# Adaptive max pooling on one core: which of 128 runs each partition loads, and how far apart the runs lie

## The chip, the cores and the metric

The kernel runs on one core of a Trainium2 chip. The metric is the device time of one execution in microseconds (us); the kernel before has a median of 334.78 us over 3 runs (334.77 to 335.02). One execution was also taken by the hardware profiler, and all views quoted here are of that one. Engines appear there as DVE (VectorE, which does the maxima), SPq and ACTq (the queues of SyncE and ScalarE, which here only start transfers) and POOL (GpSimd, which does nothing here beyond four constants). DMA stands for the core's 16 DMA engines. A load brings data from HBM (DRAM) into SBUF, a store takes results back. A KB in the profile's list of transfers is 1024 bytes, an MB in its totals is a million.

## The reference

```python
# x: (32, 256, 4096) float32, output_size = 256
for i in range(output_size):
    start = int(i * length / output_size)
    end = int((i + 1) * length / output_size)
    result[:, :, i] = np.max(x[:, :, start:end], axis=-1)
```

4096 / 256 = 16, so each output is the maximum of 16 neighbouring floats. Input and output are both contiguous, so the whole task is this: 32 * 256 * 256 = 2,097,152 windows of 64 B lie one after the other in DRAM, and the output is one float for each, in the same order. 134.2 MB are read and 8.4 MB written.

## The kernel before, in words

Each of the 128 partitions pools 2,097,152 / 128 = 16,384 windows. They are taken in two groups. Group A gives each partition 128 + 8 * 1024 + 1020 = 9340 windows, group B the other 7044. Within a group the windows are cut into 128 runs of equal length, one run per partition. In the kernel before, `group` (L66 to L73) gives partition p run p: its pattern `(p n) w -> p (n w)` makes run p begin p pitches behind the group's start, where the pitch is the length of a run, 9340 * 64 B = 597,760 B = 2335 blocks of 256 B in group A and 7044 * 64 B = 1761 such blocks in group B.

A run is loaded in pieces ("chunks"), the same piece of all 128 runs in one transfer, so that a chunk of 1024 windows is 128 rows of 64 KiB, one row for each partition. Group A is loaded from its end towards its beginning: a chunk of 128 windows first (`FIRST`, the load of L87), then eight of 1024 and one of 1020 (`CHUNK - LESS`; the loads of L96). Group B follows with six chunks of 1024 and a last one, `last`, which has 900 windows. The last chunk's length follows from `LESS`, since the two groups together must cover 16,384 windows.

The chunks go into `ring`, an SBUF buffer that holds two of them plus two gaps of 152 windows. Loads take the two halves in turn. A chunk is pooled by two instructions of `pooled` (L53 to L60, the instruction itself is on L56), one on 872 windows and one on 152; the order of the two and the gap let the next load of the same half start when the first of them is done. The maxima go into `kept`, another SBUF buffer, which holds all results but those of the last chunk; those are written into a part of `ring` (`last_kept`).

All loads are started by SP, in program order, each when the half that it fills is free. Behind the loads SP starts two stores (L117): the first with all of group A, 9340 floats per partition, the second with the first 6144 floats per partition of group B. The results of the last chunk, 900 floats per partition, are stored from the ScalarE queue (L114) when the last maximum is there. No engine's order is left to a planner here: every queue runs its instructions in the order in which the program writes them, and only semaphores make it wait.

The buffers of one transfer are given as two patterns, one for DRAM and one for SBUF. In the kernel before both count 128 rows in their outermost dimension.

## Time and profile before

| what | value |
|---|---|
| median of 3 runs | 334.78 us |
| span of the profiled execution | 333.1 us |
| DVE busy | 276.5 us, 83% of the span |
| DMA packets and bytes | 2880 packets, 142.61 MB |
| mean rate over the span | 428 GB/s |
| queue started by SP: share of 16 engines' span | 98.8% |
| queue started by ScalarE: share of 16 engines' span | 0.3% |
| mean time of a pooling instruction on 872 windows | 14.686 us |
| the same on 152 windows | 2.676 us |
| the same on the last chunk's 900 windows | 15.143 us |

The median is 1.7 us above the span of the profiled execution, since the span counts only from the first to the last instruction. The page gives each engine's busy time, a row of digits with the busy tenths in 40 equal slices of the span, the DMA queues with their share of the time of all 16 engines, the chain of work that ended last, the costliest groups of instructions with the idle time in front of them, and the transfers by the line that starts them, with the time from the start of the issuing instruction to the landing of the last byte. In that last list a transfer that stands in a queue behind others has that wait in its time.

### The profile page before, as it was taken

To read this page: it belongs to the slowest core of one execution; us is meant where nothing else is said; L and a number is where in the kernel's file an instruction comes from. 1 tells how busy PE (TensorE), PEld (TensorE's weight loads), DVE (VectorE), ACT (ScalarE), POOL (GpSimd) and SP (SyncE) were. 2 spreads that over 40 slices of the span, in tenths; PEclk is the share of its full clock that TensorE was granted. 3 is DMA by queue.
4 is the path that set the end of the run, shared out by engine and by line. 5 is a ranking of instruction groups with operands and counts; after the bars stand their busy time and mean duration, and the time that the engine had idled before them with its cause. 6 is when DMAs were issued, how large, how long until landed. Compare 5 with 4: busy or idle time off the path is not lost.

```text
span 333.1 us, 113 instructions
## 1 busy us (share of the span) xinstructions
DVE 276.5 (83%) x32; POOL 0.2 (0%) x4
## 2 busy tenths in 40 slices
DVE  2009979797997979799797979979797998979993
POOL 0000000000000000000000000000000000000000
DMA  9898989899898989899898989899898989899997
GB/s 378 378 504 378 504 378 504 378 449 433 378 504 378 504 378 504 378 441 441 384 494 377 504 378 504 378 456 425 386 496 378 504 378 504 378 458 443 393 395 330
DMA packets 2880, 142.61 MB, mean 428 GB/s; under 512 B 320, under 2 KB 320, under 8 KB 448
## 3 DMA queue, kind: packets, MB, share of 16 engines
q1 hardware_dynamic: 2736, 142.15, 98.8%
q10 hardware_dynamic: 144, 0.46, 0.3%
HBM read 134.22 MB, written 8.39 MB: 428 GB/s over the span
## 4 chain that ended last, share of the span: by engine, by line
DMA 57%; DVE 36%; DVEq 5%; issue 0%; SPq 0%
DMA ring<-in_x_dram 57%; DVE kept L56 36%; DVEq L148 5%; SPq L87 0%
## 5 line engine op out<-in xcount | busy, mean ns | idle before, releaser
L56 DVE TENSOR_REDUCE kept<-ring 128x152 f32<-128x2432 f32 (+3 forms) x31 | 261.4, 8473 | 51.5 <-DMA ring<-in_x_dram 51.5
L56 DVE TENSOR_REDUCE ring<-ring 128x900 f32<-128x14400 f32 x1 | 15.1, 15143 | 0.0
L134 POOL MEMSET const-bfloat16-1.0<- 128x1 bf16 x1 | 0.1, 103 | 0.0
L134 POOL MEMSET const-uint8-127<- 128x1 uint8 x1 | 0.1, 102 | 0.0
L134 POOL MEMSET const-float32-0.0<- 128x1 f32 x1 | 0.1, 100 | 0.2 <-issue 0.2
L134 POOL MEMSET const-float32-1.0<- 128x1 f32 x1 | 0.1, 99 | 0.0
## 6 DMA issues: line engine op xcount, KB each, us to landing
ring<-in_x_dram SPq DMA_DIRECT2D x1, 8160.0 KB, 23.9
ring<-in_x_dram SPq DMA_DIRECT2D x1, 7200.0 KB, 21.7
out_dram<-kept SPq DMA_DIRECT2D x1, 4670.0 KB, 32.4
out_dram<-kept SPq DMA_DIRECT2D x1, 3072.0 KB, 18.2
ring<-in_x_dram SPq DMA_DIRECT2D x1, 1024.0 KB, 4.7
out_dram<-ring ACTq DMA_DIRECT2D x1, 450.0 KB, 4.2
ring<-in_x_dram SPq DMA_DIRECT2D x14, 24.0
```

The costliest lines, as they stand in the source:

```text
L56: nc.vector.reduce_max(out=dst, in_=ring[:, at * W : (at + n) * W].rearrange("p (n w) -> p n w", w=W), axis=mybir.AxisListType.X,)
L134: nc = _bacc.Bacc("TRN2", target_bir_lowering=False, num_devices=1)
L148: with _tile.TileContext(nc) as tc:
```

## The change

Three things change together. `LESS` becomes 32: group A's last chunk has 992 windows in place of 1020, and the last chunk of group B has 928 in place of 900. With that a run of group A has 9312 windows, a pitch of 2328 blocks of 256 B in place of 2335, and a run of group B has 7072, a pitch of 1768 blocks in place of 1761. And `group` cuts the 128 runs into 8 sets of 16: its pattern is now `(j i n) w -> i j (n w)` with i counting 16 and j counting 8. The tile's side of each transfer still counts 128 partitions in order, so that partition 8 i + j takes run 16 j + i. Partitions 0 to 7 take runs 0, 16, 32 and so on up to 112, partition 8 takes run 1. Loads and stores both use it, so each result goes back to where its window was. `by_run` returns what it is given.

In the instructions the DRAM side of a load was 128 rows by 16384 floats; now it is 16 by 8 rows by 16384 floats, while the SBUF side is 128 by 1 by 16384. The number, order and waits of the instructions on each engine stay as they were.

```diff
-    LESS = 4
+    LESS = 32
+    RUNS = 16
...
+    def by_run(tile_rows):
+
+        return tile_rows
...
-            xw[span].rearrange("(p n) w -> p (n w)", p=P),
-            ow[span].rearrange("(p n) -> p n", p=P),
+            xw[span].rearrange("(j i n) w -> i j (n w)", i=RUNS, n=n),
+            ow[span].rearrange("(j i n) -> i j n", i=RUNS, n=n),
...
-            xn = xg[:, a * W : (a + n) * W]
+            xn = xg[:, :, a * W : (a + n) * W]
...
-                    out=ring[:, CHUNK * W : (CHUNK + n) * W], in_=xn
+                    out=by_run(ring[:, CHUNK * W : (CHUNK + n) * W]), in_=xn
...
-                nc.sync.dma_start(out=ring[:, at * W : (at + n) * W], in_=xn)
+                nc.sync.dma_start(
+                    out=by_run(ring[:, at * W : (at + n) * W]), in_=xn
+                )
...
-        stores.append((og[:, 0:full], kept[:, base : base + full]))
+        stores.append((og[:, :, 0:full], by_run(kept[:, base : base + full])))
...
-    nc.scalar.dma_start(out=og[:, full : full + last], in_=last_kept)
+    nc.scalar.dma_start(out=og[:, :, full : full + last], in_=by_run(last_kept))
```

## The prediction

> **What bounds the kernel now.** I read the page's busy tenths and queues first, to see whether an engine or the transfers fill the span.

> ```profile
> DVE  2009979797997979799797979979797998979993
> DMA  9898989899898989899898989899898989899997
> DMA packets 2880, 142.61 MB, mean 428 GB/s; under 512 B 320, under 2 KB 320, under 8 KB 448
> q1 hardware_dynamic: 2736, 142.15, 98.8%
> q10 hardware_dynamic: 144, 0.46, 0.3%
> ```

> The 16 DMA engines have something to move for 98.8 + 0.3 = 99.1% of the span; DVE has holes. The packets tell how a transfer is cut: the ScalarE queue carried one store, of 128 rows, in 144 packets, so 128 rows and 16 more, one for each engine. An engine thus has 8 rows of every transfer. Next, the table by stretches, cut where DVE's work on a chunk begins:

> ```profile
> core 0: us, DVE busy (x) POOL busy (x), PEclk, DMA share, GB/s
> 24.78:295.62 270.84, 241.84 (x28) 0.00 (x0) 1.00 1.00 433
> 312.82:327.99 15.17, 15.14 (x2) 0.00 (x0) 1.00 1.00 431
> 327.99:333.10 5.11, 0.00 (x0) 0.00 (x0) 1.00 0.59 244
> ```

> For 14 chunks on end the DMA share is 1.00 at 433 GB/s, and while only stores move (from 312.82) 1.00 at 431. So each engine moves 433 / 16 = 27.1 GB/s, into SBUF and out of it alike. Last, the waits, the timeline and the landings:

> ```profile
> DVE kept L56 <- DMA ring<-in_x_dram: 51.5, 16, 17.1
> ```

> ```profile
> 44.13 17.28 DVE L56 TENSOR_REDUCE kept<-ring 128x872 f32<-128x13952 f32 x2 [2.07 <-DMA ring<-in_x_dram]
> 63.48 17.28 DVE L56 TENSOR_REDUCE kept<-ring 128x872 f32<-128x13952 f32 x2 [2.07 <-DMA ring<-in_x_dram]
> ```

> ```profile
> ring<-in_x_dram SPq DMA_DIRECT2D x1, 1024.0 KB, 4.7
> out_dram<-ring ACTq DMA_DIRECT2D x1, 450.0 KB, 4.2
> ```

> DVE needs 17.28 us for a chunk and waits 2.07 us for the next one; chunks come every 63.48 - 44.13 = 19.35 us, which is 8,388,608 B at 433.5 GB/s. The chain of waits alternates load and DVE (57% and 36%), but that DVE share stands for no cost: a load is issued 4.6 us (19.35 - 14.70) before the one ahead of it lands, so the queue never runs dry. The bound is the DMA engines' rate. 142.61 MB at 433.5 GB/s take 329.0 us, and the other 4.1 us of the span are the start and the last landing. The median is 1.7 us above the span; I add that to every span below.

> **The change part by part.**

> *Instructions.* SP still issues 17 loads and 2 stores, ScalarE 1 store, DVE 32 poolings, in the same order with the same waits; no instruction is moved past another. Their patterns have a dimension more. The first load's issue takes 0.383 us and lies bare at the start; the others took 0.327 to 0.426. No row shows the new form's issue: at the least -0.06 us (0.327 in place of 0.383), at the most another issue's length, +0.38. I take +0.2, between them. The other loads' issues are covered by the 4.6 us of queued load; without that cover each would cost its 0.2, 3 us in all.

> *The other lengths.* 28 windows go from group A's last chunk to the last one. Poolings of 872 and 900 windows take 14.686 and 15.143, so 28 windows are 0.46 us. They leave a chunk where DVE waits anyhow, and join the last pooling. Chunks in between land 28 * 64 * 128 B / 433.5 GB/s = 0.53 us earlier, the last load where it did (312.7), and DVE then is free at 312.3 instead of 312.82: the last pooling ends at 312.7 + 15.6 = 328.3, 0.35 later. The small store behind it has room: the first load, 1 MB, landed 4.7 us from its issue, 2.4 of it for the bytes, which leaves 2.3 fixed; the small store should need 2.3 + 1.1, but took 4.2, so for 0.8 us it stood behind the big one. 0.35 and 0.2 for its own issue fit into that: 0 us. Without this cover: +0.55, or +0.73 with the issue's upper end.

> *Which engine moves which rows.* This part touches all 142.61 MB, and the DMA share of 1.00 leaves no room under it. A transfer was 128 rows outermost on both sides; now it is 16 by 8 on one and 128 on the other. An engine has 8 rows either way, but which 8 partitions those are can change. No row prices another dealing. One end is 0: all engines go on at 27.1 GB/s. For the other: that rate is the same inward and outward, so I read it as the limit of an engine's own way to SBUF, with 16 engines on 16 ways. If the dealing sends engines to a way two at a time, each gets half while they meet: 142.61 MB at 216.8 GB/s are 657.8 us, the span 661.9, the median 663.6, +329. I take a value near this upper end. Full rate on 16 ways at once needs a dealing that fits the ways, and "8 neighbouring partitions for an engine" is the plain reading of 16 against 128; that this plain dealing fits as exactly as the old one is the special case. Two engines of a pair don't start on the same instant, so at each hand-over one is briefly alone; I put 2% of the time down to that, 13 us: 650.

> [...]

> *Where the runs lie.* The places that 16 engines read at a time were several pitches apart and now may be 1 apart; the rows that one engine reads in turn go from neighbours to 16 * 595,968 B apart. No row shows addresses that hurt: odd pitches ran at the ways' limit. I take 0; the other end is again a rate between 216.8 and 433.5, at 3.3 us for each 1%.

> **Rivals.**

> 1. *The pairs drift apart.* [...] Against: nothing in the rows shows unequal engines; 14 chunks came at 19.35 us each. If they part within the first chunk or two, the loss is 20 to 40 us (19.35 for each chunk at half rate): 355 to 375. If it takes half the loads, about 500. I use 500.
> 2. *The dealing stays as good as it was; not slower.* For: the same bytes in rows of the same size, 2880 packets. It decides if no two engines meet: then nothing but the 0.2 at the start is left, 335.0 us; its bounds are 334.7 and 335.9 (+1.1: 0.38 at the start, 0.73 at the end). A gain over 0.2% has to come out of the 4.1 us outside the full rate; the first load came 4.7 - 2.4 = 2.3 us late, and 16 neighbouring runs could at most shorten that start.
> 3. *The new addresses conflict in DRAM while the ways are fine.* For: one engine's rows now lie 16 pitches apart. Against: 2328 is 8 * 291, so the 16 runs of one step still differ in their low address bits. At a 5% lower rate, 334.8 + 17 = 352 us.

> **How the numbers follow.** A measurement of this kernel can tell about 0.2%, 0.67 us, from no change (its runs spread 0.25). Chances: engines meet in pairs for most of the time 0.55 (650 us; own range 590 to 666); pairs that drift apart 0.15; rate unchanged 0.24; DRAM conflict 0.06. Of the unchanged rate, 0.15 lies within 0.67 us of 334.78, 0.05 above (issue and tail bare), 0.04 below (a better start). Slower: 0.55 + 0.15 + 0.06 + 0.05 = 0.81; same 0.15; faster 0.04. The unchanged rate holds more than 2 in 10, so the range must reach it: from 334.6 (that bound less 0.1 for the runs' own spread) to 666, where 663.6 is full pairing and the rest the issue and tail. It is wide because it spans two cases with little between.

> **What would show it.** Pairs: chunks come every 38 us and DVE waits 21 in front of each, pooling instructions unchanged at 14.69 and 2.68 us, mean rate near 217 GB/s with the DMA share still near 1.00, the last load landing late enough that its pooling is wholly beside the stores. Drift: short intervals late, long ones early. Unchanged: 433 GB/s, 2.07 us waits, the last pooling 15.6 us. Addresses: a lower rate that is even over the loads. The forecast is wrong if the new form is dealt out as the old one was, or if two engines on one way don't halve each other.

## The result and the profile after

The changed kernel takes 683.96 us (median of 6 runs, 681.7 to 685.82) against 335.04 us before in the same comparison: 2.0415 times as long, 95% interval 2.0384 to 2.0445. The profiled execution, one that took 684.99 us, has a span of 683.2 us, 0.8 us under the median.

The busy tenths and queues of the changed kernel, to be held against those of before:

```profile
DVE  1018072460906327091542708145180723609080
DMA  9989889899898898998989989899899898899997
DMA packets 2880, 142.61 MB, mean 209 GB/s; under 512 B 320, under 2 KB 320, under 8 KB 448
q1 hardware_dynamic: 2736, 142.13, 99.2%
q10 hardware_dynamic: 144, 0.48, 0.2%
```

The DMA row looks as it did, and the queues' shares still add up to 99.4%. The packets are the same 2880. Only the mean rate is another: 209 GB/s in place of 428. So the engines are not idle; each row takes longer: by the trace's records of single packets a row of 64 KiB took 2.42 us before and takes 5.12 us now (medians of 1792 rows each). A busy share of DMA says that packets are under way, not that they move at full rate: the stretches show a share of 1.00 at 433 GB/s before and at 207 here.

The same kernel by stretches (the columns are DVE, POOL, TensorE's clock, DMA share and rate): 13 chunks (one of them with 992 windows), then everything behind the last load's landing.

```profile
89.15:615.04 525.89, 224.09 (x27) 0.00 (x0) 1.00 1.00 207
651.68:683.20 31.52, 15.62 (x1) 0.00 (x0) 1.00 0.89 246
```

Three chunks and the end in the timeline, and the transfers with their time from issue to landing:

```profile
89.15 17.28 DVE L57 TENSOR_REDUCE kept<-ring 128x872 f32<-128x13952 f32 x2 [23.30 <-DMA ring<-in_x_dram]
129.70 17.28 DVE L57 TENSOR_REDUCE kept<-ring 128x872 f32<-128x13952 f32 x2 [23.27 <-DMA ring<-in_x_dram]
170.23 17.28 DVE L57 TENSOR_REDUCE kept<-ring 128x872 f32<-128x13952 f32 x2 [23.25 <-DMA ring<-in_x_dram]
...
651.68 15.62 DVE L57 TENSOR_REDUCE ring<-ring 128x928 f32<-128x14848 f32 x1 [19.37 <-DMA ring<-in_x_dram]
667.34 0.62 ACTq L121 DMA_DIRECT2D out_dram<-ring  x1
```

```profile
ring<-in_x_dram SPq DMA_DIRECT2D x1, 1024.0 KB, 7.3
out_dram<-ring ACTq DMA_DIRECT2D x1, 464.0 KB, 15.0
```

DVE still needs 17.28 us for a chunk, but waits 23.3 us in front of each in place of 2.07. Chunks come every 40.5 us (170.23 - 129.70) in place of 19.35, and they keep that pace from the second chunk to the last. The time went into the loads: the last one lands at 651.7 us in place of 312.7, 339 us later. What comes behind it, the last pooling and the stores, takes 31.5 us in place of 20.4. The two together are 350.1 us, and the spans differ by 683.2 - 333.1 = 350.1.

### The profile page after: what moved, and what is told of

Its sections match the earlier page's. It is cut to its first block, busy times and chain, and to the rows that moved or that the text cites. A ratio compares the mean times of both kernels' runs of the same rounds, so it can differ in the third digit from the quotient of the medians.

```text
span 683.2 us, 113 instructions
## 1 busy us (share of the span) xinstructions
DVE 276.6 (40%) x32; POOL 0.2 (0%) x4
## 2 busy tenths in 40 slices
DMA packets 2880, 142.61 MB, mean 209 GB/s; under 512 B 320, under 2 KB 320, under 8 KB 448
## 3 DMA queue, kind: packets, MB, share of 16 engines
q1 hardware_dynamic: 2736, 142.13, 99.2%
HBM read 134.22 MB, written 8.39 MB: 209 GB/s over the span
## 4 chain that ended last, share of the span: by engine, by line
another core or an unknown queue 50%; DVE 40%; DMA 7%; SPq 0%; issue 0%; DVEq 0%
DVE kept L57 38%; DMA ring<-in_x_dram 7%; DVE ring L57 2%; SPq L92 0%; DVEq L57 0%
## 5 line engine op out<-in xcount | busy, mean ns | idle before, releaser
L57 DVE TENSOR_REDUCE ring<-ring 128x928 f32<-128x14848 f32 x1 | 15.6, 15620 | 19.4 <-DMA ring<-in_x_dram 19.4
## 6 DMA issues: line engine op xcount, KB each, us to landing
ring<-in_x_dram SPq DMA_DIRECT2D x1, 1024.0 KB, 7.3
```

Of the source, the lines that this page charges most:

```text
L57: nc.vector.reduce_max(out=dst, in_=ring[:, at * W : (at + n) * W].rearrange("p (n w) -> p n w", w=W), axis=mybir.AxisListType.X,)
```

## The experiments

My theory, called "dealing" in the expectations: the shape of 16 by 8 rows against 128 gives each DMA engine 8 neighbouring partitions, and engines then meet in pairs on their way into SBUF: two share one way, and each gets about half of its rate. No record names the engine that moved a row, so which engine serves which partitions, and which engines share a way, can only be inferred from rates and row times: "way", "pair" and "sharing" are my reading of those, here and below. The rivals put the loss on the DRAM side: "pitch", the new distance between runs, and "order", an engine's rows lying 16 runs apart. The change has all three in it, so I took it apart first.

### The pitches alone, and the order alone

The kernel before, with the new lengths:

```diff
-    LESS = 4
+    LESS = 32
```

> The kernel before with LESS = 32: pitches of 2328 and 1768 blocks, partition p takes run p, both sides count 128 rows. Theory 'dealing' (the 16 by 8 shape makes the 16 engines meet in pairs on their way into SBUF): chunks every 19.35 us, 334.8 to 335.4 us (at most 0.35 from the longer last pooling). Theory 'pitch' (multiples of 8 blocks conflict in DRAM): most of the 349 us lost by the change, so over 600 us. Theory 'order' (an engine's rows lie 16 pitches apart): about 335 us.

Measured: 334.84 us against 335.0, ratio 0.9996 (0.9986 to 1.0005). The new pitches cost nothing. The sum's small terms can be read here too: the last pooling has 928 windows, and the small store behind it landed after 3.7 us in place of 4.2, so the longer pooling was indeed covered by the time for which that store had stood in the queue.

The changed kernel with the old lengths:

```diff
-    LESS = 32
+    LESS = 4
```

> The changed kernel with LESS = 4: the old pitches of 2335 and 1761 blocks, partition 8 i + j takes run 16 j + i, 16 by 8 rows against 128. 'Dealing': chunks every 40.6 us as in the changed kernel, 684 us. 'Pitch': back to 335 us. 'Order': about 684 us.

Measured: 684.14 us, ratio 2.0419 (2.0378 to 2.046), a chunk every 40.5 us. Its loads by stretches:

```profile
48.56:615.32 566.76, 241.84 (x28) 0.00 (x0) 1.00 1.00 207
```

So the whole loss comes from the 16 by 8 pattern, which still means two things: where an engine's rows lie in DRAM, and which partitions it serves.

### The same scatter with another outermost count

```diff
-    RUNS = 16
+    RUNS = 32
```

> The changed kernel with RUNS = 32: partition 4 i + j takes run 32 j + i, pitches of 2328 and 1768 blocks, 32 by 4 rows against 128. [...] 'Order' and 'pitch': still near 684 us.

Measured: 335.64 us, ratio 1.003 (1.0016 to 1.0043). The stretch of 14 chunks, in the columns used above:

```profile
25.58:296.82 271.24, 241.37 (x28) 0.00 (x0) 1.00 1.00 432
```

Neighbouring partitions still read runs that lie 32 pitches apart, with the pitches of the changed kernel, and the rate is back at 432 GB/s. So this scatter alone does not slow the loads. Which partitions an engine then serves is not shown; with "dealing" the rate fits if no two engines meet. With `RUNS = 64`:

```diff
-    RUNS = 16
+    RUNS = 64
```

> The changed kernel with RUNS = 64: partition 2 i + j takes run 64 j + i, 64 by 2 rows against 128, pitches 2328 and 1768. With RUNS = 32 the time was 0.3% above before, of which 0.28 us is the longer issue of the first load (0.66 in place of 0.38 us). [...] 'Order': engines' rows up to 64 pitches apart, slower than with 32 runs.

Measured: 335.51 us, ratio 1.0019 (1.001 to 1.0028), with the loads at full rate:

```profile
25.36:295.87 270.51, 241.38 (x28) 0.00 (x0) 1.00 1.00 433
```

Both stand a little above before. The issue of the first load, bare at the start, is part of that; the first line below is of before, the second of this kernel, start and length in us:

```profile
0.73 0.38 SPq L87 DMA_DIRECT2D ring<-in_x_dram  x1
```

```profile
0.73 0.67 SPq L92 DMA_DIRECT2D ring<-in_x_dram  x1
```

That is 0.29 us of the 0.55 by which the medians differ; the rest was not followed further.

### Fewer engines

```diff
-    RUNS = 16
+    RUNS = 8
```

> The changed kernel with RUNS = 8: partition 16 i + j takes run 8 j + i, 8 by 16 rows against 128. If an outermost count of 8 leaves 8 engines, each alone at 27.1 GB/s would make 217 GB/s and about 664 us. 'Dealing': 16 neighbouring partitions for each of 8 engines, and these meet in pairs again: half of the changed kernel's rate, chunks every 81 us, about 1360 us. 'Order' and 'pitch' have no reason for a second doubling: 684 us, or 664 if only the engines count.

Measured: 1295.05 us, in one run. The page, the stretch of 14 chunks, and three chunks from the beginning, the middle and the end:

```profile
DMA packets 2720, 142.61 MB, mean 110 GB/s; under 512 B 160, under 2 KB 160, under 8 KB 288
q1 hardware_dynamic: 2584, 142.13, 49.7%
```

```profile
92.52:1174.06 1081.54, 241.37 (x28) 0.00 (x0) 1.00 0.50 109
```

```profile
171.92 17.28 DVE L57 TENSOR_REDUCE kept<-ring 128x872 f32<-128x13952 f32 x2 [62.12 <-DMA ring<-in_x_dram]
...
643.42 17.28 DVE L57 TENSOR_REDUCE kept<-ring 128x872 f32<-128x13952 f32 x2 [60.91 <-DMA ring<-in_x_dram]
...
1174.06 17.28 DVE L57 TENSOR_REDUCE kept<-ring 128x872 f32<-128x13952 f32 x2 [57.64 <-DMA ring<-in_x_dram]
```

The queue's share is 49.7% of 16 engines and there are 160 packets fewer, 8 for each of the 20 transfers: with this outermost count of 8, 8 engines move the rows. Eight engines at the 27.1 GB/s that each moved before would make 217 GB/s; these make 109. So, by the rate, they meet as well. It is 5% faster than I expected, and the waits show why: they fall steadily, from 62.12 to 57.64 us. The packet records fit the drift of my first rival, pairs getting out of step little by little: in the first load of 1024 windows the shortest quarter of the rows took 4.75 us on average and the others 5.10, in the last such load 3.79 and 4.98. In the changed kernel the shortest quarter stays at 4.93 to 4.94 us from the first such load to the last. Why the pairs drift with 8 engines and not with 16 stays open.

### Neighbouring rows in DRAM, dealt the new way

The kernel before, with its loads put into 16 by 8 form by hand. The step between the sets of eight is 4 windows short, so that the two counts do not amount to one count of 128 at equal steps:

```diff
-            xw[span].rearrange("(p n) w -> p (n w)", p=P),
+            bass.AP(
+                x.tensor,
+                (taken - n) * P * W,
+                [[(8 * n - 4) * W, 16], [n * W, 8], [1, n * W]],
+            ),
...
-            xn = xg[:, a * W : (a + n) * W]
+            xn = xg[:, :, a * W : (a + n) * W]
```

> The kernel before, its loads alone put into the 16 by 8 shape with runs all but where they were: partition 8 i + j reads run 8 i + j, set 60 i windows at most 3.75 KB per set towards the front (a step of 8 runs less 4 windows between the sets of eight), so that the two dimensions don't fold into one; an output then is that of a window up to 60 places further on. Stores as before. 'Dealing': chunks every 40.5 us, all loads at half rate, stores at the old rate: 8.1 at the first chunk's landing, 15 chunks, then 18.6 for the stores and 1.7, about 669 us. 'Order' (rows 16 pitches apart): 335 us, since an engine's rows are neighbours here.

Measured: 673.44 us, ratio 2.0101 (2.0043 to 2.0159). From the timeline and the stretches:

```profile
89.37 17.28 DVE L56 TENSOR_REDUCE kept<-ring 128x872 f32<-128x13952 f32 x2 [23.29 <-DMA ring<-in_x_dram]
129.94 17.28 DVE L56 TENSOR_REDUCE kept<-ring 128x872 f32<-128x13952 f32 x2 [23.29 <-DMA ring<-in_x_dram]
```

```profile
652.16:672.30 20.14, 15.15 (x1) 0.00 (x0) 1.00 0.89 381
```

A chunk every 40.57 us, with rows that are neighbours in DRAM and within 3.75 KB of where they were. The order of the runs is out as a cause; the loads' 16 by 8 shape halves the rate without it, to 207 GB/s. With the stores in the old form the end is back at 20.1 us.

### The stores alone

```diff
-            ow[span].rearrange("(p n) -> p n", p=P),
+            ow[span].rearrange("(j i n) -> i j n", i=16, n=n),
...
-        stores.append((og[:, 0:full], kept[:, base : base + full]))
+        stores.append((og[:, :, 0:full], kept[:, base : base + full]))
...
-    nc.scalar.dma_start(out=og[:, full : full + last], in_=last_kept)
+    nc.scalar.dma_start(out=og[:, :, full : full + last], in_=last_kept)
```

> The kernel before with the stores alone in the new shape: loads as before (partition p loads run p), but its results go to the place of run 16 j + i of partition 8 i + j, so outputs stand in another order. 'Dealing': loads every 19.35 us, then 8.39 MB of stores that took 18.4 us from the last load's landing take between 18.4 and twice that; in the changed kernel 30 us passed from there to the end, so about 347 us, 355 at the most. If stores didn't suffer from the dealing, 335.

Measured: 350.22 us, ratio 1.0453 (1.0423 to 1.0484). Loads, then stores, by stretches:

```profile
24.64:295.47 270.83, 241.84 (x28) 0.00 (x0) 1.00 1.00 433
312.69:348.20 35.51, 15.16 (x2) 0.00 (x0) 1.00 0.91 219
```

The loads run as before; from the last load's landing to the end it takes 35.5 us in place of 20.4. The stores suffer from the new shape as the loads do, but by less than a doubling. In the changed kernel nearly the same stores cost 31.5 us, 4 less than here. The packet records show where the difference lies. Each row of the first store (about 36 KB) took 1.38 us before, and again in the kernel with 32 runs, whose results are scattered too. Here the median is 2.82 us, but 15% of the rows took under 1.5; in the changed kernel the median is 1.79 us and 31% took under 1.5. So part of the stores' rows ran as if alone, more of them behind paired loads. Why they do was not settled.

### The way belongs to the partitions

The test that separates "engines meet on their way into SBUF" from causes on the DRAM side: one program twice, with the base partition as the only difference. If ways belong to partitions, the two times can differ; if the cause lies in DRAM, they are the same. It loads 64 of the 128 runs as 16 by 4 rows. The core of the edit to the kernel before:

```diff
+    LOW = 0        # 32 in the twin
...
-            xw[span].rearrange("(p n) w -> p (n w)", p=P),
+            xw[span].rearrange("(h j i n) w -> h i j (n w)", h=2, i=16, n=n)[0],
...
-                nc.sync.dma_start(out=ring[:, at * W : (at + n) * W], in_=xn)
+                nc.sync.dma_start(
+                    out=ring[LOW : LOW + 64, at * W : (at + n) * W], in_=xn
+                )
```

> Half of the work: only runs 0 to 63 of each group are loaded, into partitions 0 to 63, as 16 by 4 rows (partition 4 i + j takes run 16 j + i); of each chunk only the first 128 windows are pooled, and three blocks of 128 results per partition are stored. Same rows in DRAM as in the twin below. 'Dealing', with ways that belong to partitions: if 0 to 31 and 32 to 63 share their ways, 8 ways serve 16 engines: chunks of 4 MB every 20.3 us (half of 40.57), about 320 us in all. If each engine has a way of its own whatever the partitions: every 9.7 us, about 162 us.

> The same instructions on the same DRAM rows, but into partitions 32 to 95. [...] 'Order' or anything else on the DRAM side: the same time as the twin.

Measured, in one run each: 339.61 us into partitions 0 to 63, 167.57 us into partitions 32 to 95. By stretches, 14 chunks of each:

```profile
26.50:312.86 286.36, 63.69 (x28) 0.00 (x0) 1.00 1.00 205
```

```profile
14.41:149.91 135.50, 63.73 (x28) 0.00 (x0) 1.00 1.00 432
```

### What sharing costs beyond the halves

The same kernel on the first 16 runs and partitions, one row per engine and load. The line of the load's pattern, against the kernel with 64 runs (the tile's side shrinks with it):

```diff
-            xw[span].rearrange("(h j i n) w -> h i j (n w)", h=2, i=16, n=n)[0],
+            xw[span].rearrange("(h i n) w -> h i (n w)", h=8, i=16, n=n)[0],
```

> One eighth of the work: only runs 0 to 15 of each group, into partitions 0 to 15, one 64 KiB row per engine and load; 128 windows of each chunk are pooled and stored. Measured before: two engines that share a way all the time take 5.119 us for a row each, 2.56 us of the way per row, against 2.418 for an engine alone (5.9% more). If partitions 0 to 3 share one way, 4 engines share it here. Theory 'a toll for taking turns at all': 4 * 2.56 = 10.24 us per load, 16 loads, about 166 us. Theory 'a toll for each further engine' (5.9% for the second, as much again for the third and fourth): 4 * 2.418 * 1.18 = 11.4 us, about 184 us. No toll: 9.67 us, 157 us.

Measured: 162.93 us, in one run. Two loads of it:

```profile
33.20 2.27 DVE L60 TENSOR_REDUCE kept<-ring 16x128 f32<-16x2048 f32 x1 [7.36 <-DMA ring<-in_x_dram]
42.83 2.27 DVE L60 TENSOR_REDUCE kept<-ring 16x128 f32<-16x2048 f32 x1 [7.36 <-DMA ring<-in_x_dram]
```

A load every 9.63 us, 1,048,576 B at 109 GB/s, which is four times an engine's 27.1. If that is 4 ways with four of the 16 engines on each, as the rate suggests, there is no toll, against both theories. (The total lies between the sums, which had too little for the start and the end; the interval of the loads decides.) Then the first 32 runs and partitions, 16 by 2 rows:

```diff
-            xw[span].rearrange("(h j i n) w -> h i j (n w)", h=2, i=16, n=n)[0],
+            xw[span].rearrange("(h j i n) w -> h i j (n w)", h=4, i=16, n=n)[0],
```

> A quarter of the work: only runs 0 to 31 of each group, into partitions 0 to 31, as 16 by 2 rows, so two rows per engine and load; 128 windows of each chunk are pooled and stored. Measured: two sharers of a way lost 5.9% on top of their halves (64 partitions from 0), four sharers on partitions 0 to 15 lost nothing (9.64 us for four rows). Theory 'it is the number': two per way again, 4 * 2.56 = 10.24 us per load, about 167 us. [...]

Measured: 174.02 us, in one run. Two loads:

```profile
35.85 2.27 DVE L60 TENSOR_REDUCE kept<-ring 32x128 f32<-32x2048 f32 x1 [7.97 <-DMA ring<-in_x_dram]
46.09 2.27 DVE L60 TENSOR_REDUCE kept<-ring 32x128 f32<-32x2048 f32 x1 [7.97 <-DMA ring<-in_x_dram]
```

A load every 10.24 us, to the hundredth what "it is the number" asked for. (The total is 7 us above my 167: I had counted 16 loads and too little for the start and the end.) Two sharers need 5.7 to 5.9% more time than the halving alone would give, four need none beyond their quarter; how many share is read from the rates. Why two don't fill a way that one or four do is not known from these runs.

No variant that moves all the bytes beats the kernel before: the pitches alone equal it, 32 and 64 runs stand 0.2 to 0.3% above it, and the others are clearly slower.

## Why the prediction was right and where it was wrong

The direction held: the rate about halves, from 433 to 207 GB/s, with the DMA share still at 1.00. The mechanism, engines that meet in pairs on the way into SBUF, was not seen itself, but the runs fit it: a row of 64 KiB took 5.12 us in place of 2.42, and the partitions that are written decide between 205 and 432 GB/s. The size was short: 683.96 us measured, against 650 and a range that ended at 666.

- *The failed step* is in "Which engine moves which rows": "each gets half while they meet: 142.61 MB at 216.8 GB/s are 657.8 us". I treated this as the upper end, as if sharing could cost nothing by itself. Into partitions 0 to 63, where by the row times pairs share all the time, the engines moved 205 GB/s, not 216.8, and the changed kernel's loads 207. A chunk took 40.55 us on average where the half rate asks for 38.70: 1.85 us more, and over the loads' 16 chunks' worth of bytes that is 29.6 us. This term alone carries the time past my range.
- *The 2% for hand-overs* had the right sign and was too large. No row of before showed this term; it was my estimate, and that one engine of a pair is briefly alone is not shown. What the packet records show: in the changed kernel the first 16 rows of each load of 1024 windows start within 0.91 to 0.95 us of one another, and a quarter of the rows took 4.93 us and the others 5.12, while at base 0 no row was under 5.04. Eight rows that are shared all the time would be 8 * 5.11 = 40.9 us; the chunk took 40.55, 0.9% less.
- *The stores* were in the same term at half rate. Between the last load's landing and the end the half rate asks for 20.4 + 19.4 = 39.8 us; it took 31.5, 8.3 less. Together: 661.9 + 29.6 - 8.3 = 683.2, which is the measured span.
- *The instructions.* I took +0.2 us for the first load's issue; it went from 0.383 to 0.657 us, +0.27. The later issues were covered, as stated: the load queue never ran dry.
- *The other lengths* cost nothing, by the cover that I named: the kernel with the pitches alone is at 0.9996 of before.
- *Where the runs lie* was taken at 0. The runs with 32 and 64 sets, whose rows are as scattered, stand 0.2 to 0.3% above before, issue included.
- *The rivals.* Drift of the pairs did not come with 16 engines: no chunk from the second on was shorter than its 40.5 us, but for the one that has 992 windows. It showed only with 8 engines. A dealing as good as the old one exists, at outermost counts of 32 and 64, but not at 16. The DRAM conflict fell with the neighbouring rows, which were as slow, and with the two programs that differ in the base partition.

My prediction put the half rate at the end of the range because the formula gave nothing beyond it. But if a way carries no more than the 27.1 GB/s of one engine, half the rate is the most that two sharers can reach, so it bounds the time of paired transfers from below, and the range had no room above it.

## What to carry to other kernels

Where the DMA share is 1.00, look at how a transfer's two patterns deal its rows to the engines, and not only at its bytes and addresses: against 128 partitions, DRAM patterns with 32, 64 or 128 rows outermost ran at 432 to 433 GB/s, 16 at 207 and 8 at 109. A tile on 64 partitions ran at 205 GB/s from partition 0 and at 432 from partition 32. Read the rate beside the share, since the share was the same at 207 and at 433. And when a cost is bounded by "they take turns", leave room for what taking turns costs itself: here 5.7 to 5.9% of the time, beyond the halving.

## What was not expected

- Where by the rates two engines share a way into SBUF, they took 5.7 to 5.9% longer for their rows than one alone would for both (5.11 us a row for each, in place of twice 2.42); where by the rates four share one, they took no longer (9.63 us for four rows, in place of four times 2.42).
- Paired stores were slowed less than paired loads: 35.5 us against 20.4 for the end of the kernel, and 31.5 behind paired loads; 15% and 31% of the first store's rows ran as if alone.
- With 8 engines the loads got faster over the run: the wait in front of a chunk fell from 62.1 to 57.6 us.
- A pattern with one dimension more made the issue of the first load 0.27 us longer (0.383 to 0.657).
